# Attention inside one hybrid decoder layer on one core: the sink as a score column, earlier copies of transposed weights, one block without Strassen

## The chip, the cores and the metric

The kernel runs on one core of one Trainium2 chip. The metric is the device time of one execution in microseconds (us), lower is better.

## The reference

One layer of a decoder trunk for 512 tokens of width 1024, all in float32. An input projection feeds two branches, sliding-window attention (A) and gated linear attention (GLA, B); gates mix them; a SwiGLU block and a per-layer embedding block follow. The part that the change touches is A, with 8 query heads in 2 groups, 128-token blocks and a window of 128, and the projection of q and k for B:

```python
q_a, k_a, v_a, q_g, k_g, v_g, gk_low, og, gate_a, gate_g = jnp.split(h @ w_in, points, axis=-1)
...
s = jnp.einsum('bnqhgd,bnkhd->bnhgqk', qb, kb) * (HEAD_DIM ** -0.5)
s = s + band_relative_bias(rel_table)
dist = (jnp.arange(BLOCK)[:, None] + BLOCK) - jnp.arange(2 * BLOCK)[None, :]
in_window = (dist >= 0) & (dist < WINDOW)
...
s = jnp.where(valid[None, :, None, None], s, -1e30)
m = jnp.maximum(jnp.max(s, axis=-1, keepdims=True), sink)
pr = jnp.exp(s - m)
denom = jnp.sum(pr, axis=-1, keepdims=True) + jnp.exp(sink - m)
o = jnp.einsum('bnhgqk,bnkhd->bnqhgd', pr / denom, vb)
```

The sink is one number per head that joins the maximum and the denominator and has no value vector. A query at place q of its block sees the keys of the block before at places above q only, so the first key of the block before (column 0 of 256) is outside the window for every query.

## The kernel before

Matmuls run in three products of fp32r halves: `split` makes a high part (`_h`, a CAST on ACT, line 111) and a low part (`_l`, a TENSOR_TENSOR on DVE or POOL, line 112), and `mm3` (lines 122 to 124) issues high by high, low by high, high by low. Weights arrive by DMA from the SP queue into four raw tiles, are split into four slots (`wh`, `wl`) and are used in the order of the list `units`.

Two ways to multiply a block of 256 output columns by the 1024 inputs and 512 tokens exist. `fm_pair` is the plain one: 2 output halves by 8 input tiles by 3 matmuls of 512 tokens. `quad_pair` is Strassen's scheme in Winograd's form: seven quarter products of 4 by 3 matmuls of 256 tokens, named by four parts .0 to .3, with sums of weight quarters made on POOL (`sums_to`, line 237; tiles `qk0.0s`, `qk1.0s`, two tiles per block in two buffers) and with sums of the activation quarters `h_t` made once on DVE and ACT for all blocks. One running PSUM bank (`qk0pa`) collects the products; after each part ACT copies it to SBUF (`copy`, line 549; tiles `qk0u`, `qk0v`), and the next part's matmuls into that bank wait for that copy. DVE adds the pieces (line 545). The q and k of GLA are the blocks qk0 to qk3, its output gate the blocks og0 to og3.

Attention (`attention`, from line 714) has eight items j (block n of four, group g of two). Each is cut in steps: `scores` (matmuls into `sc`, two evictions with scale and bias on DVE into `s_all`, then the softmax), `transposes` (four or eight on PE into `pt`, one or two copies on ACT to `pT`), `values` (matmuls into `pov`). The softmax of an item is, in order: maximum of the scores (`mx`, DVE line 746), minimum of its negative with the negated sink (`nm`, 749), sink plus that (`dl`, 751), its exponential (`es`, ACT 753), four exponentials of the scores with sums (`su`, ACT 756), sum plus `es` (`de`, DVE 758), reciprocal (`rd`, 760), four scalings (ACT 762).

The steps are interleaved by hand: `drive(gla_qk(), att)` advances attention by one step after each quarter part of a qk block, `drive(gla_gate((0, 1)), att)` goes on with og0 and og1. A scheduler then sets the order of each engine's queue from program order and its own estimates; each engine runs its queue strictly in that order. `high_priority` puts an instruction ahead in that scheduler's eyes. Ahead of qk0 on all engines stand the attention queries' blocks qa0 and qa1, whose low parts for the two groups are tiles `qa<-qa,qs` (DVE for group 0, POOL for group 1), copied by DMA to `qs`.

```python
    att = attention()
    drive(gla_qk(), att)
    drive(gla_gate((0, 1)), att)
```

Of the kernel before, what the change touches and what calls it, by code (L numbers as in the profile page):

```python
# [9 lines left out]
F32 = mybir.dt.float32  # L10
F32R = mybir.dt.float32r
U8 = mybir.dt.uint8
AF = mybir.ActivationFunctionType
ALU = mybir.AluOpType
AX = mybir.AxisListType

P = 128
S = 512
D = 1024
NT = S // P  # L20
KD = D // P
# [6 lines left out]
C_QG, C_KG, C_VG = 768, 1280, 1792  # L28
# [5 lines left out]
def hybrid_layer(  # L34
# [26 lines left out]
    nc = tc.nc  # L61
    x = x[0]
    out = out[0]
# [10 lines left out]
    sm = ctx.enter_context(tc.tile_pool(name="sm", bufs=4))  # L74
# [11 lines left out]
    def t2(name, shape=(P, 512), dt=F32):  # L86
        return tp.tile(list(shape), dt, tag="t2", name=name)
# [54 lines left out]
    def u_rows(name, mat, k0, n, c0, ncol=512, per=2):  # L142

        for u in range(n // per):
            k = k0 + per * u
            units.append((f"{name}{u}", (per, ncol), [((ALL,), mat[:, k : k + per, c0 : c0 + ncol])]))
# [16 lines left out]
    for i in range(2):  # L163
        for kh in range(2):
# [2 lines left out]
                c0 = C_QA + (4 * g + 2 * i) * 64  # L167
                pieces.append(((ALL, ALL, slice(128 * g, 128 * g + 128)), wk[:, 4 * kh : 4 * kh + 4, c0 : c0 + 128]))
            units.append((f"qa{i}{kh}", (4, 256), pieces))
    for i in range(4):  # L170
        u_quad(f"qk{i}", wk, C_QG + 256 * i)
    for i in range(4):
        u_quad(f"og{i}", wk, C_OG + 256 * i)
# [296 lines left out]
    bgk = cpool.tile([P, 4], F32, name="bgk")  # L470
    glag = cpool.tile([P, 2], F32, name="glag")
    sink = cpool.tile([P, 8], F32, name="sink")
    nsink = cpool.tile([P, 8], F32, name="nsink")
    rt = cpool.tile([32, 8], F32, name="rt")
    oh = t2("oh")
    band = t2("band")
# [15 lines left out]
    with tc.issue_after(done):  # L492
        nc.vector.tensor_copy(rts, rt.unsqueeze(1).broadcast_to([32, 16, 8]))
        nc.vector.tensor_scalar_mul(glag, glag, 0.5)
        nc.vector.tensor_scalar_mul(nsink, sink, -1.0)
        nc.vector.tensor_scalar_mul(nbgk, bgk, -1.0)
        nc.vector.tensor_copy(masks, mraw)

# [82 lines left out]
    def fm_pair(name, act, evac):  # L581

        pss = [bank(f"{name}p{x}") for x in "ab"]
        for kh in range(2):
            w = W.take(f"{name}{kh}")
            for e in range(2):
                fm_mms(pss[e], w, tok(e), act, 4 * kh, 4, kh == 0, kh == 1)
                if kh:
                    evac(e, pss[e])
                yield  # L590
# [124 lines left out]
    def attention():  # L715
        items = [(n, g) for n in range(NT) for g in range(2)]
        pov = {}
        pTs = {}

        def spans(n):  # L720
            nk = 1 if n == 0 else 2
            return nk, nk * P, (n + 1 - nk)

        def scores(j):
            n, g = items[j]
            nk, w, kb = spans(n)
            rows = slice(64 * g, 64 * g + 64)
            s = s_all[:, j % 2, :, :w]
            for pair in range(2):
                ps = bank(f"sc{j}{pair}").rearrange("p (a b) -> p a b", a=2)  # L730
                keys = slice(kb * P, (n + 1) * P)
                for a in range(2):
                    h = 2 * pair + a
                    if n == 0:
                        nc.tensor.matmul(ps[:, a, :w], lhsT=qa[rows, h, tok(n)], rhs=k_aT[rows, 0:P], start=True, stop=True)
                        continue
                    q = qs[g][:, h, tok(n)]
                    nc.tensor.matmul(ps[:, a, :w], lhsT=q, rhs=ks[g][:, keys], start=True, stop=False)
                    nc.tensor.matmul(ps[:, a, :w], lhsT=q, rhs=kl[g][:, keys], start=False, stop=True)
                hs = slice(g * 4 + 2 * pair, g * 4 + 2 * pair + 2)  # L740
                nc.vector.scalar_tensor_tensor(
                    out=s[:, 2 * pair : 2 * pair + 2, :], in0=ps[:, :, :w], scalar=0.125, in1=bias[:, hs, 256 - w : 256],
                    op0=ALU.mult, op1=ALU.add,
                )
            mx = sm.tile([P, 4], F32, tag="mx", name=f"mx{j}")
            nc.vector.tensor_reduce(out=mx, in_=s, axis=AX.X, op=ALU.max, negate=True)
            sk = sink[:, 4 * g : 4 * g + 4]
            nm = sm.tile([P, 4], F32, tag="nm", name=f"nm{j}")
            nc.vector.tensor_tensor(out=nm, in0=mx, in1=nsink[:, 4 * g : 4 * g + 4], op=ALU.min)  # L749
            dl = sm.tile([P, 4], F32, tag="dl", name=f"dl{j}")  # L750
            nc.vector.tensor_tensor(out=dl, in0=sk, in1=nm, op=ALU.add)
            es = sm.tile([P, 4], F32, tag="es", name=f"es{j}")
            nc.scalar.activation(es, dl, AF.Exp)
            su = sm.tile([P, 4], F32, tag="su", name=f"su{j}")
            for a in range(4):
                nc.scalar.activation(s[:, a, :], s[:, a, :], AF.Exp, bias=nm[:, a : a + 1], accum_out=su[:, a : a + 1])  # L756
            de = sm.tile([P, 4], F32, tag="de", name=f"de{j}")
            nc.vector.tensor_add(de, su, es)
            rd = sm.tile([P, 4], F32, tag="rd", name=f"rd{j}")
            nc.vector.reciprocal(rd, de)  # L760
            for a in range(4):
                nc.scalar.activation(s[:, a, :], s[:, a, :], AF.Copy, scale=rd[:, a : a + 1])  # L762

        def transposes(j):
            n, g = items[j]
            nk, w, kb = spans(n)
            s = s_all[:, j % 2, :, :w]
            pTs[j] = []
            for b in range(nk):
                pst = bank(f"pt{j}{b}")  # L770
                for a in range(4):
                    nc.tensor.transpose(out=pst[:, tok(a)], in_=s[:, a, tok(b)], identity=ident)
                pT = t2(f"pT{j}{b}")
                nc.scalar.copy(pT, pst)  # L774
                pTs[j].append(pT)

        def values(j):
            n, g = items[j]
            nk, w, kb = spans(n)
            rows = slice(64 * g, 64 * g + 64)  # L780
            if g == 0:
                pov[n] = bank(f"pov{n}")
            for b in range(nk):
                nc.tensor.matmul(  # L784
                    pov[n][rows, :], lhsT=v_a[:, kb + b, rows], rhs=pTs[j][b], start=(b == 0), stop=(b == nk - 1)
                )
            del pTs[j]
            if g:
                split(oaT.part(0, ALL, tok(n)), pov[n].rearrange("p (t q) -> p t q", t=4))

        for j in range(len(items) + 1):
            if j < len(items):
                scores(j)
                yield
            if j == 1:

                yield
            if j:
                transposes(j - 1)
                yield  # L800
                values(j - 1)
                if j != 2:
                    yield
# [4 lines left out]
    sild = dram.tile([8, P, 512], F32, name="sild")  # L808

    def gla_qk():  # L810
        for i in range(4):
            yield from quad_pair(f"qk{i}", hT, [kq[i % 2][:, e, 1 - i // 2, :] for e in range(2)], lambda e: None)

    def gla_gate(pairs):
# [548 lines left out]
```

## Time and profile before

| | |
|---|---|
| Median of 3 runs | 885.09 us (883.25, 885.09, 885.2) |
| The profiled execution: its time, and its span | 883.18 us, 881.4 us |
| PE busy (matmul) | 855.3 us, 97% of the span |
| PEld (weight load, beside PE) | 751.7 us, 85% |
| DVE busy | 580.0 us, 66% |
| ACT busy | 454.4 us, 52% |
| POOL busy | 256.1 us, 29% |
| Mean granted TensorE clock | 0.996 of full speed |
| Chain that ended last, by engine | PE 79%, DVE 11%, ACT 4%, issue 3% |

A busy share is the mean of stages with different limits. A wait is put to whichever engine released it last. Matmuls overlap, so the distance between the starts of two matmuls in a row, not the duration of one, is what each costs. Idle time of an engine that no one waits for costs nothing.

### The profile page before, as it was taken

The numbers are of one execution on the slowest core, as the hardware profiler recorded it, in microseconds if no ns is written. First come the engines' busy times: TensorE is split into PE (matmuls) and PEld (weight loads), VectorE is DVE, ScalarE is ACT, GpSimd is POOL, SyncE is SP. The second block draws the span as 40 slices with busy tenths as digits, with TensorE's granted clock in tenths as the row PEclk, the third lists the DMA queues.
The fourth block names the chain that finished last, engine by engine and source line by source line (L and its number), as shares of the span: only waits on it lengthen the run. The fifth ranks groups of instructions, "written<-read, shape, count | busy, mean of one in ns | idle before, by whom it ended". The sixth has DMA issues, their size and how long they took to land.

```text
span 881.4 us, 15106 instructions
## 1 busy us (share of the span) xinstructions
PE 855.3 (97%) x5937; PEld 751.7 (85%) x5937; DVE 580.0 (66%) x840; ACT 454.4 (52%) x898; POOL 256.1 (29%) x211
## 2 busy tenths in 40 slices
PE   9999989999999999999998999999999999999996
PEld 7977887879777788888887999889999889998886
DVE  5534986669876634256378899535998436984574
ACT  6337767766755544333255655314555314553553
POOL 4333574331111200100033465024662034620001
PEclk9999999999999999999999999999999999999999
DMA  9482332234654337874214233431333423343402
GB/s 279 125 207 83 114 109 73 72 109 127 197 180 156 121 120 239 290 259 143 96 48 168 89 103 97 144 96 50 100 114 100 141 73 96 93 144 123 168 1 95
DMA packets 88246, 113.30 MB, mean 129 GB/s; under 512 B 6152, under 2 KB 64304, under 8 KB 87792
## 3 DMA queue, kind: packets, MB, share of 16 engines
q1 hardware_dynamic: 86704, 107.43, 38.4%
q0 software_dynamic: 1456, 4.92, 2.0%
q8 instruction: 46, 0.75, 0.3%
q14 instruction: 24, 0.20, 0.1%
q10 hardware_dynamic: 16, 0.00, 0.0%
HBM read 95.35 MB, written 15.93 MB: 126 GB/s over the span
## 4 chain that ended last, share of the span: by engine, by line
PE 79%; DVE 11%; ACT 4%; issue 3%; DMA 1%; SPq 1%; POOL 0%; POOLq 0%; DVEq 0%; ACTq 0%
DVE u L1242 2%; PE pov L784 1%; PE lv L877 1%; DVE h_t L112 1%; PE yaps L122 1%; PE yaps L124 1%; PE gt0ps L122 1%; PE gt0ps L124 1%; PE wo0ps L122 1%; PE yaps L123 1%; PE fo00ps L122 1%; PE fo10ps L123 1%; PE gt0ps L123 1%; PE wo0ps L124 1%; PE wo0ps L123 1%
## 5 line engine op out<-in xcount | busy, mean ns | idle before, releaser
L308 POOL TENSOR_TENSOR or<-om,mhalf 128x1 f32<-128x1 f32 x16 | 12.3, 770 | 64.7 <-DVE om L312 64.7
L111 ACT CAST act_h<-u 128x512 fp32r<-128x512 f32 x22 | 13.7, 621 | 27.4 <-DVE u L1242 27.4
L1242 DVE TENSOR_TENSOR u<-u,g 128x512 f32<-128x512 f32 x22 | 25.7, 1169 | 0.4
L869 DVE TENSOR_TENSOR zs<-zs,kq 128x512 f32<-128x512 f32 x28 | 19.8, 723 | 5.8 <-ACT zs L865 5.8
L308 POOL TENSOR_TENSOR h20r<-h20n,mhalf 128x1 f32<-128x1 f32 x1 | 0.6, 562 | 72.1 <-DVE h20n L317 72.1
L961 ACT ACTIVATE own<-o,or 128x256 f32<-128x256 f32 x16 | 7.6, 475 | 18.6 <-POOL or L308 18.5
L784 PE MATMUL pov<-pT,kv 128*64 128x512 f32 x28 | 14.4, 612 | 2.9 <-ACT pT L774 2.9
L756 ACT ACTIVATE s_all<-s_all,nm 128x256 f32<-128x256 f32 (+1 forms) x32 | 15.1, 472 | 3.2 <-DVE nm L749 3.2
L863 DVE TENSOR_TENSOR zs<-G 128x512 f32<-128x512 f32 x24 | 15.8, 684 | 0.4 <-DMA G<-Gd 0.4
L762 ACT ACTIVATE s_all<-s_all,rd 128x256 f32<-128x256 f32 (+1 forms) x32 | 13.2, 473 | 5.4 <-DVE rd L760 5.3
L112 DVE TENSOR_TENSOR act_l<-u,act_h 128x512 fp32r<-128x512 f32 x22 | 14.9, 680 | 0.0
L1239 ACT ACTIVATE g<-g 128x512 f32<-128x512 f32 x22 | 13.9, 631 | 0.3
L122 PE MATMUL yaps<-qs,pa_h 128*128 128x512 f32 x32 | 13.6, 426 | 0.0
L864 ACT ACTIVATE zs<-zs 128x256 f32<-128x256 f32 x28 | 11.7, 419 | 3.6 <-DVE zs L863 3.2
L111 ACT CAST mx_h<-yg 128x512 fp32r<-128x512 f32 x8 | 5.0, 622 | 15.5 <-DVE yg L1077 15.5
L122 PE MATMUL v1ps<-v_h,h_h 128*128 128x512 f32 x32 | 12.9, 403 | 0.0
L122 PE MATMUL gt0ps<-gt_h,xT_h 128*128 128x512 f32 x32 | 12.9, 402 | 0.0
L122 PE MATMUL wo0ps<-wo_h,mx_h 128*128 128x512 f32 x32 | 12.7, 395 | 0.0
L122 PE MATMUL wo1ps<-wo_h,mx_h 128*128 128x512 f32 x32 | 12.6, 394 | 0.0
L124 PE MATMUL yaps<-qs,pa_l 128*128 128x512 f32 x32 | 12.6, 394 | 0.0
L124 PE MATMUL gt0ps<-gt_h,xT_l 128*128 128x512 f32 x32 | 12.5, 391 | 0.0
L124 PE MATMUL v1ps<-v_h,h_l 128*128 128x512 f32 x32 | 12.5, 390 | 0.0
(2556 smaller groups left out, 3680.7 us busy)
## 6 DMA issues: line engine op xcount, KB each, us to landing
mg<-mgd SPq DMA_DIRECT2D x8, 512.0 KB, 5.8
vd<-v_g SPq DMA_DIRECT2D x2, 1024.0 KB, 4.8
sild<-gw SPq DMA_DIRECT2D x8, 256.0 KB, 2.1
own<-vd SPq DMA_DIRECT2D x4, 512.0 KB, 5.3
own<-sild SPq DMA_DIRECT2D x4, 512.0 KB, 5.1
mgd<-gw SPq DMA_DIRECT2D x8, 256.0 KB, 2.4
ogd<-og SPq DMA_DIRECT2D x8, 256.0 KB, 3.8
mgd<-sgg SPq DMA_DIRECT2D x8, 256.0 KB, 3.9
```

The costliest lines, as they stand in the source:

```text
L111: ins = nc.scalar.copy(hi, src)
L112: eng.tensor_tensor(out=lo, in0=src, in1=hi.bitcast(F32), op=ALU.subtract)
L122: nc.tensor.matmul(ps, lhsT=l[0], rhs=r[0], start=first, stop=False, **kw)
L123: nc.tensor.matmul(ps, lhsT=l[0], rhs=r[1], start=False, stop=False, **kw)
L124: nc.tensor.matmul(ps, lhsT=l[1], rhs=r[0], start=False, stop=last, **kw)
L756: nc.scalar.activation(s[:, a, :], s[:, a, :], AF.Exp, bias=nm[:, a : a + 1], accum_out=su[:, a : a + 1])
L762: nc.scalar.activation(s[:, a, :], s[:, a, :], AF.Copy, scale=rd[:, a : a + 1])
L784: nc.tensor.matmul(pov[n][rows, :], lhsT=v_a[:, kb + b, rows], rhs=pTs[j][b], start=(b == 0), stop=(b == nk - 1))
L863: pe.tensor_tensor(out=z3, in0=g3, in1=g3[:, :, b - 1 : b].broadcast_to([P, nb, 2 * b]), op=ALU.subtract)
L869: nc.vector.tensor_tensor(out=d4, in0=d4, in1=kq_, op=ALU.mult)
L1239: nc.scalar.activation(gs[e], gs[e], AF.Silu)
L1242: nc.vector.tensor_tensor(out=us[e], in0=us[e], in1=gs[e], op=ALU.mult)
```

## The change

Three edits, all in the code around attention.

The sink becomes one more column of the scores: it is copied into `s_all` (column 0, which the window always masks, or column 128 for the first block, which has 128 keys), so the maximum and the exponentials' sums take it in. `nsink`, `mx`, `dl`, `es` and `de` go, and with them four DVE instructions and one on ACT per item, and one DVE copy of 128x4 comes. Since column 0 then holds a probability, the values of the block before are taken from `v_z`, a copy of `v_a` with row 0 zeroed, made once on POOL.

The copies `pT` get priority 300. The block qk0 is multiplied by `fm_pair` in place of `quad_pair`; its evacuations are two copies on ACT.

```diff
-    for i in range(4):
+    u_rows("qk0", wk, 0, KD, C_QG, 256, 4)
+    for i in range(1, 4):
         u_quad(f"qk{i}", wk, C_QG + 256 * i)
...
-    nsink = cpool.tile([P, 8], F32, name="nsink")
...
+        v_z = t2("v_z", (P, NT, P))
+        nc.gpsimd.tensor_copy(v_z, v_a)
+        nc.gpsimd.memset(v_z[0:1], 0.0)
...
-            mx = sm.tile([P, 4], F32, tag="mx", name=f"mx{j}")
-            nc.vector.tensor_reduce(out=mx, in_=s, axis=AX.X, op=ALU.max, negate=True)
-            sk = sink[:, 4 * g : 4 * g + 4]
+            at = 0 if nk == 2 else w
+            nc.vector.tensor_copy(s_all[:, j % 2, :, at], sink[:, 4 * g : 4 * g + 4])
+            s = s_all[:, j % 2, :, : max(w, at + 1)]
             nm = sm.tile([P, 4], F32, tag="nm", name=f"nm{j}")
-            nc.vector.tensor_tensor(out=nm, in0=mx, in1=nsink[:, 4 * g : 4 * g + 4], op=ALU.min)
-            dl = sm.tile([P, 4], F32, tag="dl", name=f"dl{j}")
-            nc.vector.tensor_tensor(out=dl, in0=sk, in1=nm, op=ALU.add)
-            es = sm.tile([P, 4], F32, tag="es", name=f"es{j}")
-            nc.scalar.activation(es, dl, AF.Exp)
+            nc.vector.tensor_reduce(out=nm, in_=s, axis=AX.X, op=ALU.max, negate=True)
...
-            de = sm.tile([P, 4], F32, tag="de", name=f"de{j}")
-            nc.vector.tensor_add(de, su, es)
             rd = sm.tile([P, 4], F32, tag="rd", name=f"rd{j}")
-            nc.vector.reciprocal(rd, de)
+            nc.vector.reciprocal(rd, su)
...
-                nc.scalar.copy(pT, pst)
+                with tc.high_priority(offset=300):
+                    nc.scalar.copy(pT, pst)
...
-                    pov[n][rows, :], lhsT=v_a[:, kb + b, rows], ...
+                    pov[n][rows, :], lhsT=(v_z if b < nk - 1 else v_a)[:, kb + b, rows], ...
...
     def gla_qk():
-        for i in range(4):
+        yield from fm_pair("qk0", hT, lambda e, ps: nc.scalar.copy(kq[0][:, e, 1, :], ps))
+        for i in range(1, 4):
```

The order of the queues moves between about 84 and 197 us of the span; after og1 it is the same as before on every engine. Three places matter below.

POOL, from the low part of the attention keys to the sums of qk2; `qk1.0s` are the sums for block qk1, `qk1.0_l` and `qk0.3_l` low parts of weights, `qa` the low parts of the queries of group 1. Before:

```order
L237 TENSOR_TENSOR qk1.0s_930<-qk1r_812,qk1r_852 128x512
L112 TENSOR_TENSOR qa<-qa,qs_889 64x2x384
L237 TENSOR_TENSOR qk1.0s_930<-qk1.0s_930,qk1r_812 128x512
L112 TENSOR_TENSOR qk0.3_l<-qk0r_741,qk0.3_h 128x512
L237 TENSOR_TENSOR qk1.0s_931<-qk1r_852,qk1.0s_930 128x512
L237 TENSOR_TENSOR qk1.0s_931<-qk1r_812 128x512
L112 TENSOR_TENSOR qa<-qa,qs_889 64x2x384
```

Now:

```order
L720 COPY v_z<-kv 128x512
L721 MEMSET v_z 1x512
L238 TENSOR_TENSOR qk1.0s_840<-qk1r_804,qk1r_838 128x512
L238 TENSOR_TENSOR qk1.0s_841<-qk1r_804 128x512
L238 TENSOR_TENSOR qk1.0s_840<-qk1.0s_840,qk1r_804 128x512
L238 TENSOR_TENSOR qk1.0s_841<-qk1r_838,qk1.0s_840 128x512
L112 TENSOR_TENSOR qk1.0_l<-qk1r_838,qk1.0_h 128x512
L112 TENSOR_TENSOR qa<-qa,qs_887 64x2x384 x2
```

All of qk0's own work has left POOL, the sums of qk1 stand together, and the queries' low parts come behind them.

ACT, from the split of the second pair of queries (`qs`) to the copy `pT` of the first item. Before:

```order
L756 ACT_TABLE_LOAD
L756 ACTIVATE s_all,su_1027<-s_all,nm_1021 128x128
L753 ACTIVATE es_1025<-dl_1023 128x4
L756 ACTIVATE s_all,su_1027<-s_all,nm_1021 128x128 x3
L111 CAST qk1.1_h<-qk1.0s_930 128x1024
L762 ACTIVATE s_all<-s_all,rd_1034 128x128 x3
L549 COPY qk0v<-qk0pa 128x256
```

Now:

```order
L111 CAST qk1.1_h<-qk1.0s_840 128x1024
L111 CAST qs_886<-qa 64x2x384
L111 CAST qs_887<-qa 64x2x384
L756 ACT_TABLE_LOAD
L756 ACTIVATE s_all,su_1004<-s_all,nm_1002 128x129 x4
L111 CAST qk1.2_h<-qk1.0s_841 128x1024
L760 ACTIVATE s_all<-s_all,rd_1009 128x128 x4
L756 ACTIVATE s_all,su_1038<-s_all,nm_1036 128x129 x4
L810 COPY kq_965<-qk0pa 128x512
L760 ACTIVATE s_all<-s_all,rd_1043 128x128 x4
L810 COPY kq_965<-qk0pb 128x512
L773 COPY pT_1090<-pt_1085 128x512
```

The cast `qk1.1_h`, which reads a sum that POOL makes, now stands ahead of the first item's whole softmax, and no copy of the running bank stands among the scalings.

ACT around the copies `pT` of the fifth item (pt_1697 and pt_1704 before, pt_1595 and pt_1602 now), whose reader is the value product. Before:

```order
L111 CAST og0.2_h<-og0.0s_1522 128x1024
L756 ACTIVATE s_all,su_1647<-s_all,nm_1641 128x256
L753 ACTIVATE es_1645<-dl_1643 128x4
L756 ACTIVATE s_all,su_1647<-s_all,nm_1641 128x256 x2
L549 COPY kq_974<-qk3pa 128x256
L774 COPY pT_1702<-pt_1697 128x512
L774 COPY pT_1709<-pt_1704 128x512
```

Now:

```order
L111 CAST og0.2_h<-og0.0s_1427 128x1024
L773 COPY pT_1600<-pt_1595 128x512
L773 COPY pT_1607<-pt_1602 128x512
L756 ACTIVATE s_all,su_1547<-s_all,nm_1545 128x256 x2
L548 COPY kq_966<-qk3pa 128x256
```

The two copies moved ahead of the next item's exponentials.

## Rows read from the trace of the kernel before

**Rows 1.** Waits of PE, whole span: us in total, times, longest.

```profile
PE qk0pa L122 <- ACT qk0v L549: 3.2, 1, 3.2
PE pov L784 <- ACT pT L774: 2.9, 2, 1.6
PE fg00pc L122 <- DVE h2t L1110: 2.1, 1, 2.1
...
PE pt L772 <- ACT s_all L762: 0.9, 1, 0.9
```

**Rows 2.** Busy time by stretch: PE, PEld, DVE, ACT, POOL, clock, DMA.

```profile
110.00:132.00 22.00, 19.52 (x135) 17.63 (x136) 19.05 (x27) 14.80 (x43) 16.94 (x13) 0.92 0.37 111
...
462.00:484.00 22.00, 18.60 (x120) 16.52 (x119) 19.05 (x26) 12.43 (x24) 6.86 (x5) 1.00 0.52 176
```

**Rows 3.** Timeline of PE, qa1 to qk1: start, duration, instruction, [idle before].

```profile
87.07 0.39 PE L122 MATMUL qa1pa<-h_h,qa_h 128*128 128x512 f32 x1
...
97.95 0.28 PE L122 MATMUL qk0pa<-h_h,qk0.0_h 128*128 128x256 f32 x1
...
100.70 0.28 PE L124 MATMUL qk0pb<-h_h,qk0.0_l 128*128 128x256 f32 x1
...
112.47 0.39 PE L122 MATMUL qk0pa<-h_t,qk0.3_h 128*128 128x256 f32 x1 [3.19 <-ACT qk0v L549]
...
118.93 1.07 PE L784 MATMUL pov<-pT,kv 128*64 128x512 f32 x2
119.94 0.38 PE L122 MATMUL qk1pa<-h_t,qk1.1_h 128*128 128x256 f32 x1
```

**Rows 4.** Timeline of ACT, same stretch.

```profile
96.73 1.69 ACT L111 CAST qs<-qa 64x768 fp32r<-64x768 f32 x2
...
104.12 1.28 ACT L756 ACT_TABLE_LOAD   x1
...
108.34 0.39 ACT L756 ACTIVATE s_all<-s_all,nm 128x128 f32<-128x128 f32 x1
...
109.49 1.03 ACT L111 CAST qk1.1_h<-qk1.0s 128x1024 fp32r<-128x1024 f32 x1
111.18 0.99 ACT L762 ACTIVATE s_all<-s_all,rd 128x128 f32<-128x128 f32 x3 [0.66 <-DVE rd L760]
```

**Rows 5.** Timeline of DVE, same stretch.

```profile
99.88 1.21 DVE L112 TENSOR_TENSOR qk0.2_l<-qk0.0s,qk0.2_h 128x1024 fp32r<-128x1024 f32 x1
101.06 1.98 DVE L112 TENSOR_TENSOR qa<-qa,qs 64x768 fp32r<-64x768 f32 x1
...
106.13 0.69 DVE L746 TENSOR_REDUCE mx<-s_all 128x4 f32<-128x512 f32 x1
...
109.62 1.05 DVE L758 TENSOR_TENSOR de<-su,es 128x4 f32<-128x4 f32 x1 [0.76 <-ACT s_all L756]
```

**Rows 6.** Timeline of POOL, same stretch.

```profile
84.88 1.29 POOL L112 TENSOR_TENSOR qk0.0_l<-qk0r,qk0.0_h 128x512 fp32r<-128x512 f32 x1 [11.96 <-ACT qk0.0_h L111]
98.17 4.06 POOL L237 TENSOR_TENSOR qk1.0s<-qk1r,qk1r 128x512 f32<-128x512 f32 x1 [12.00 <-ACT qs L111]
...
109.38 1.27 POOL L237 TENSOR_TENSOR qk1.0s<-qk1r 128x512 f32<-128x512 f32 x1
```

**Rows 7.** Groups by line and form, 84 to 205 us: busy us, mean ns, idle.

```profile
L741 DVE SCALAR_TENSOR_TENSOR s_all<-sc,bias 128x256 f32<-128x256 f32 x4 | 1.6, 406 | 0.0
```

**Rows 8.** Timeline of PE, the fifth and the seventh item's value products.

```profile
162.70 1.93 PE L784 MATMUL pov<-pT,kv 128*64 128x512 f32 x4 [1.59 <-ACT pT L774]
...
189.41 1.07 PE L784 MATMUL pov<-pT,kv 128*64 128x512 f32 x2 [1.26 <-ACT pT L774]
```

**Rows 9.** Timeline of ACT up to the fifth item's two copies.

```profile
158.78 1.05 ACT L111 CAST og0.2_h<-og0.0s 128x1024 fp32r<-128x1024 f32 x1 [0.99 <-PE qk3pb L123]
...
162.07 1.05 ACT L774 COPY pT<-pt 128x512 f32<-128x512 f32 x2
```

**Rows 10.** Instructions that write dcy, a DVE copy of 128x4: duration min/median/max ns.

```profile
L913 DVE COPY dcy<-eg x4: 160/162/1007, 208.6 to 281.0; 128x4 f32<-128x4 f32 x4
```

More of the change, by code (lines that the diff above doesn't have):

```diff
@@ L494, in hybrid_layer @@
         nc.vector.tensor_scalar_mul(glag, glag, 0.5)
-        nc.vector.tensor_scalar_mul(nsink, sink, -1.0)
         nc.vector.tensor_scalar_mul(nbgk, bgk, -1.0)
@@ L756, in scores @@
                 nc.scalar.activation(s[:, a, :], s[:, a, :], AF.Exp, bias=nm[:, a : a + 1], accum_out=su[:, a : a + 1])
-            de = sm.tile([P, 4], F32, tag="de", name=f"de{j}")
-            nc.vector.tensor_add(de, su, es)
             rd = sm.tile([P, 4], F32, tag="rd", name=f"rd{j}")
-            nc.vector.reciprocal(rd, de)
+            nc.vector.reciprocal(rd, su)
             for a in range(4):
-                nc.scalar.activation(s[:, a, :], s[:, a, :], AF.Copy, scale=rd[:, a : a + 1])
+                nc.scalar.activation(s[:, a, :w], s[:, a, :w], AF.Copy, scale=rd[:, a : a + 1])
         def transposes(j):
@@ L784, in values @@
                 nc.tensor.matmul(
-                    pov[n][rows, :], lhsT=v_a[:, kb + b, rows], rhs=pTs[j][b], start=(b == 0), stop=(b == nk - 1)
+                    pov[n][rows, :], lhsT=(v_z if b < nk - 1 else v_a)[:, kb + b, rows], rhs=pTs[j][b], start=(b == 0), stop=(b == nk - 1)
                 )
```

## The prediction

> **What bounds the kernel now.** The page says that PE is busy for 97% of the span, so a change shortens the run only by taking work off PE or by taking away a time in which PE stands. The list of waits shows where it stands [rows 1]: the longest is 3.2 us before the last part of qk0, then two waits of the value products, 2.9 us in all, and 0.9 us before a transpose. All of these lie in the stretch that the change rewrites. The timelines give their places: the 3.19 us end at 112.47 [rows 3], the value products wait 1.59 and 1.26 us [rows 8], which with the 0.9 make 6.9 us.
>
> The first wait has a second price. The table by stretch shows a granted clock of 0.92 between 110 and 132 us [rows 2]: part of it ran at the lower of the two levels, 1.2 in place of 2.4 GHz. That is (1 - 0.92) x 22 = 1.76 us of work lost right behind the 3.19 us wait. Between 462 and 484 us PE stands 22 - 18.6 = 3.4 us in several waits, the longest 2.1 [rows 1, 2], and the clock there is 1.00: not every wait of this kind is followed by the lower level.
>
> Why did PE wait? ACT had the copy of the running bank (`qk0v`) behind three scalings that began at 111.18 after 0.66 us of waiting for `rd` [rows 4]. That came behind `de`, which took 1.05 us on DVE [rows 5] for four numbers per partition. These small DVE instructions with two inputs are long where POOL works at the same time: the one at 109.62 lasts as long as the sum that POOL began at 109.38 [rows 5, 6].
>
> **qk0 plainly: more columns.** 48 matmuls of 512 tokens replace 84 of 256. The 48 of qa1 take from 87.07 to 97.95, 10.88 us. The first 24 of qk0 start from 97.95 to 100.70, so one of 256 costs 2.75 / 23 = 0.1196 us and 84 cost 10.05 [rows 3]. PE pays **+0.83 us**. Score matmuls and the switches between kinds of matmul stay as many. The running bank goes, and with it the 3.19 us wait (3.35 by the starts, since a gap of 0.12 would be normal) and, if nothing as long replaces it, the 1.76 us of lower clock: **-5.1 us** gross.
>
> **What is late next.** The order of ACT and POOL moves in a way that gives some of it back. The cast `qk1.1_h` now stands ahead of the second pair of query casts, the table load and the first softmax, and needs the third of POOL's sums for qk1. When does POOL make them? In the trace of before its first such sum is open from 98.17 and lasts 4.06 us, where an undisturbed one lasts 1.27 [rows 6]: it got through only about 101, when DVE paused between two instructions [rows 5]. In the change DVE has the same chain of two-input instructions up to about 101.2 (weights, sums of activations, a query part; it was busy to 101.06 before [rows 5]), and then itself waits for `qk1.1_h`. So I take POOL's start there. Step by step, with durations of [rows 4 to 7]: three sums at 1.27, 105.0; `qk1.1_h` 1.03, 106.0; two query casts 1.69, 107.7, while DVE waits out POOL's fourth sum, makes `qk1.1_l` (1.2) and the second query part (0.9, the 1.98 of [rows 5] less a sum's hold) until 108.3; two evictions at 0.41 and the maximum at 0.69, 109.7; the table load ended at 109.0 and is hidden; four exponentials at (109.49 - 108.34) / 3 = 0.38, 111.2; `qk1.2_h`, 112.2; four scalings at 0.33, 113.5.
>
> PE meanwhile: 97.95 + 10.88 + 2.5 for two groups of scores = 111.3 (before, 112.47 - 3.19 - 97.95 = 11.33 us held 72 matmuls of qk0, 8.6, the same two groups, and 0.2 of a last matmul's tail [rows 3]). So the first transposes wait for the scalings, about **+2.2 us**, and end at 113.8; 24 matmuls of qk1, 116.7. ACT goes on with four exponentials (115.0), a copy of 0.52 (half of the 1.05 in [rows 9]), four scalings and a second copy, then `pT` at 117.9: the first value product waits **+1.2 us**, runs 1.0 and lets qk1.1 start at 118.9. Before it started at 119.94 [rows 3]. This part therefore gains **1.0 us**, of the 5.1, if the clock holds; 2.2 us of standing is nearer to the 2.1 without a lower clock behind it than to the 3.19 with one, so I take it to hold.
>
> **The later items.** `pT` priority: at the fifth item the copies came at 162.07, behind the next item's exponentials, and PE waited 1.59 us [rows 8, 9]. They now stand ahead of them, right behind a cast that ends at 159.83 [rows 9], so they can end at 160.9, and PE comes at 161.1: the wait goes. The seventh item has the same pattern, and its 1.26 us go. At the third item the transposes waited 0.9 us for scalings that waited for `rd`; without `de`, and with the reciprocal ahead of the next maximum, some 0.2 is left. Value products that were issued one by one (1.07 each [rows 3], with work between) now come in pairs, 1.93 per pair [rows 8]: 0.2 for each of three items. Sum **-4.1 us**.
>
> **Edits at nothing.** The dropped `nsink`, `dl`, `es` and qk0's adds ease DVE and ACT, which are less busy than PE. `v_z` and its memset fall into the 12 us in which POOL idles before 84.88 [rows 6]; if POOL were late there, each would cost 1.3. The sink's copy is a DVE copy of 128x4; the four in GLA take from 0.16 to 1.01 us [rows 10]. I take 0.2, the median's end, since it stands where POOL has mostly finished its sums; at 1.0 it would return most of the third item's 0.7, and nothing elsewhere, where the scalings have over 2 us in hand. Past og1 the order is unchanged and PE has no wait that the change touches, so what is gained by then is kept to the end.
>
> **Sum.** -1.0 - 4.1 = **-5.1 us** against the profiled execution's 883.18, or 878.1. Of the four executions shown two lie near 883.2 and two near 885.1, the median 885.09 is one of the upper. From their middle, 884.15, the forecast is **879.0 us**.
>
> **Rivals.**
> - *POOL comes earlier* (20%). If DVE pauses once or twice between 95 and 101 us, the sums for qk1 are ready before ACT asks. Then no wait of 2.2 at the transposes and little at the value product: the first part gains 3.35 + 1.76 - 0.83 - 0.5 = 3.8. For it: POOL's queue is free of qk0. Against: the 4.06 us [rows 6]. 876.2 us.
> - *The clock falls again* (15%), behind a wait of 2.2 to 3 us at the first transposes: 1.76 us more, 880.8.
> - *The later waits only move* (12%). ACT's freed time is filled by exponentials that now come behind `pT`, and scalings or the copies of running banks come late in their turn; half of the 4.1 us is lost and some of the first part: 881.5 to 882.5.
> - *POOL takes its turn after every DVE instruction* (8%), slower than before. From about 96 us its four sums, a weight part and two query parts (1.27 to 1.8 each, 9.9 us) would stand between the nine DVE instructions ahead of the first eviction, which then comes at 113.5 in place of 108.3. The first transposes end at about 119 and not 113.8, the clock falls with so long a wait (1.8 or more), and qk1.1 starts near 125 plus that, 7 us later than before; less 4.1 that is 887. It decides from the point at which the first scalings end after 117. Against it: the sum open at 98.17 was passed by the DVE instruction of 99.88 [rows 5, 6].
>  The Trainium skill (SBUF — State Buffer, "Who interferes with whom") says that issue order decides which of DVE and GpSimd blocks when both want the shared port pair. Read as a strict order of requests, it would have given the port to the sum opened at 98.17 ahead of the instruction of 99.88; the trace shows otherwise. By that reading the result would be this rival's 887, by the row the forecast's 879.0.
>
> That the change does not do what it says is no case here: the order of the queues shows all three edits.
>
> **How the numbers follow.** The forecast has 45%. Its own bounds are 877 to 881 (the sink's copy, the waits of 2.2 and 1.2 by 1 us each way, the two groups of executions). About 0.3% (2.65 us) is what a measurement of this kernel can tell from no change; faster by more needs under 882.4 against the median shown. Forecast, earlier POOL, the second clock fall and part of the moved waits lie below: 0.80. The rest of the moved waits, 0.12. Slower: 0.08. The range 875.0 to 882.5 leaves out the slow rival, and the tails of the others.
>
> **What would show it.** PE's list of waits should have no `qk0pa`; in its place a wait of about 2 us at the first `pt` and one of about 1 us at the first `pov`, and none above 0.5 at later `pov`. The stretch 110 to 132 should show a clock of 1.00. ACT's cast `qk1.1_h` should start near 105 and be released by POOL. qk1.1 should start near 118.9, and og2 some 5 us earlier than before. The forecast is wrong if the first scalings end before 111.5 (better) or after 115 (worse), or if a lower clock shows.

## The result and the profile after

The changed kernel takes 877.85 us in the median of four runs (877.11 to 878.55), the kernel before 885.05 beside it: 0.9935 of the time, with a 95% interval of 0.9923 to 0.9947. The forecast was 879.0 in a range of 875.0 to 882.5. The profiled execution took 877.55 us with a span of 875.7, against 883.18 and 881.4. Three of the four executions of the kernel before lie between 885.0 and 885.2 and one at 883.25, so the medians are 7.2 us apart and the two profiled executions 5.6.

The first part of the page, busy time, share of the span and instructions:

```profile
PE 854.3 (98%) x5901; PEld 749.2 (86%) x5901; DVE 569.8 (65%) x818; ACT 450.3 (51%) x885; POOL 251.9 (29%) x207
```

PE's waits after, which answer to [rows 1] (us in total, times, longest), between 90 and 330 us:

```profile
PE pov L783 <- ACT pT L773: 1.0, 1, 1.0
PE o L953 <- ACT sc L968: 0.7, 1, 0.7
PE pt L770 <- ACT s_all L760: 0.7, 1, 0.7
```

The 3.2 us before `qk0pa`, the 2.9 in two waits at later value products and the 0.9 at later transposes are gone. What stays (`pt` and `pov`) is at the first item, and one wait is new: a value product `o` of a linear attention head, far behind the change. By stretch, as [rows 2]:

```profile
110.00:132.00 22.00, 20.34 (x143) 17.31 (x142) 14.38 (x21) 16.96 (x50) 15.61 (x11) 1.00 0.41 109
132.00:154.00 22.00, 22.00 (x160) 18.81 (x159) 13.56 (x21) 17.50 (x45) 9.85 (x7) 1.00 0.26 72
```

The clock between 110 and 132 is 1.00 in place of 0.92, and in the stretch behind it PE is busy without a gap. PE's timeline at the first item, as [rows 3]:

```profile
112.40 1.21 PE L770 MATMUL pt<-ident,s_all 128*128 128x128 f32 x4 [0.70 <-ACT s_all L760]
...
117.42 1.07 PE L783 MATMUL pov<-pT,kv 128*64 128x512 f32 x2 [0.95 <-ACT pT L773]
```

ACT, DVE and POOL there, as [rows 4 to 6]:

```profile
103.16 1.05 ACT L111 CAST qk1.1_h<-qk1.0s 128x1024 fp32r<-128x1024 f32 x1 [3.06 <-POOL qk1.0s L238]
...
111.95 1.27 ACT L760 ACTIVATE s_all<-s_all,rd 128x128 f32<-128x128 f32 x4
```

```profile
96.58 1.22 DVE L112 TENSOR_TENSOR qk_l<-qk01r,qk_h 128x1024 fp32r<-128x1024 f32 x1
97.93 2.10 DVE L112 TENSOR_TENSOR h_t<-hr,h_t 128x1024 fp32r<-128x1024 f32 x1
99.95 2.03 DVE L112 TENSOR_TENSOR qa<-qa,qs 64x768 fp32r<-64x768 f32 x1
...
103.61 1.32 DVE L750 COPY s_all<-sink 128x4 f32<-128x4 f32 x2
...
107.95 0.74 DVE L744 SCALAR_TENSOR_TENSOR s_all<-sc,bias 128x256 f32<-128x256 f32 x2
```

```profile
95.96 2.98 POOL L238 TENSOR_TENSOR qk1.0s<-qk1r,qk1r 128x512 f32<-128x512 f32 x1 [38.71 <-DMA qk1r<-in_w_in]
98.91 2.26 POOL L238 TENSOR_TENSOR qk1.0s<-qk1r 128x512 f32<-128x512 f32 x1
101.14 1.99 POOL L238 TENSOR_TENSOR qk1.0s<-qk1.0s,qk1r 128x512 f32<-128x512 f32 x1
```

From 97.8 us POOL's sums and DVE's two-input instructions take turns: the three DVE instructions shown first end at 97.80, 100.03 and 101.98, and the sums 1.14 us behind each, at 98.94, 101.17 and 103.13. A sum is open for 2 to 3 us where an undisturbed one lasts 1.27 [rows 6], and a DVE instruction of the size of the one at 96.58 grows from 1.22 to 2.10.

**A ledger of PE.** The starts of four matmuls in PE's timeline cut every profiled execution into stretches: the first of qk1.1, of og2, of ga3 (a gate's block, behind the new wait) and of wo0 (the output projection). From ga3 to wo0 all thirteen profiles have 112.0 us, and they differ behind wo0 too, with the clock, as the end of this document shows. So the start of wo0, not the span, is the sharper measure of what an edit did in the execution that was profiled; it is used below beside the times. It is one execution of each kernel, and not always a typical one. Where qk1 is plain there is no qk1.1.

| kernel | qk1.1 | to og2 | og2 to ga3 | wo0 |
|---|---|---|---|---|
| before | 119.94 | 77.59 | 102.49 | 412.03 |
| changed | 118.42 | 72.43 | 103.50 | 406.35 |
| changed, again (c_after) | 118.47 | 72.42 | 103.82 | 406.71 |
| plain qk0 alone (e1) | 122.42 | 77.46 | 102.51 | 414.41 |
| without plain qk0 (e2) | 120.77 | 72.44 | 102.50 | 407.71 |
| without priority (e3) | 118.17 | 73.74 | 102.52 | 406.43 |
| without sink column (e4) | 122.27 | 73.36 | 103.59 | 411.24 |
| sink column alone (e7) | 121.26 | 74.65 | 102.46 | 410.37 |
| qk1 plain too (e5) | | og2 at 189.16 | 103.39 | 404.56 |
| own late (e6) | 118.78 | 72.43 | 102.86 | 406.07 |
| e5 and e6 together (e8) | | og2 at 189.01 | 103.39 | 404.40 |
| the same without priority (e9) | | og2 at 189.79 | 103.55 | 405.35 |
| e1 with es late (e10) | 120.39 | 75.66 | 102.51 | 410.57 |

The change gained 1.52 us up to qk1.1, 5.16 from there to og2, and gave back 1.01 before ga3: 5.67 in all.

### The profile page after: what moved, and what is told of

It reads as the page before. It is cut to its first block, busy times and chain, and to the rows that moved or that the text cites. A ratio compares the mean times of both kernels' runs of the same rounds, so it can differ in the third digit from the quotient of the medians.

```text
span 875.7 us, 14980 instructions
## 1 busy us (share of the span) xinstructions
PE 854.3 (98%) x5901; PEld 749.2 (86%) x5901; DVE 569.8 (65%) x818; ACT 450.3 (51%) x885; POOL 251.9 (29%) x207
## 4 chain that ended last, share of the span: by engine, by line
PE 79%; DVE 9%; issue 4%; ACT 4%; DMA 2%; POOL 1%; SPq 1%; POOLq 0%; DVEq 0%; ACTq 0%
DVE u L1242 2%; PE pov L783 2%; PE v1ps L122 1%; PE gt0ps L124 1%; PE v1ps L123 1%; PE wo0ps L124 1%; PE gt0ps L122 1%; PE v1ps L124 1%; PE gt0ps L123 1%; PE fo10ps L122 1%; PE fo00ps L122 1%; PE wo0ps L122 1%; PE fo10ps L123 1%; PE fo00ps L123 1%; PE wo0ps L123 1%
## 5 line engine op out<-in xcount | busy, mean ns | idle before, releaser
L238 POOL TENSOR_TENSOR qk1.0s<-qk1r,qk1r 128x512 f32<-128x512 f32 x1 | 3.0, 2984 | 38.7 <-DMA qk1r<-in_w_in 38.7
```

## The experiments

Times are medians, each beside the kernel before on the same chip (883.39 us for e1 to e4, 884.24 for c_after and e5 to e7, 883.30 for e8 to e10), ratios with their 95% intervals.

### Which edit pays: e1, e2, e3, e4, e7

**e1**, of the diff above only the plain block:

```diff
-    for i in range(4):
+    u_rows("qk0", wk, 0, KD, C_QG, 256, 4)
+    for i in range(1, 4):
         u_quad(f"qk{i}", wk, C_QG + 256 * i)
...
```

> The kernel before with qk0 multiplied plainly and nothing else. Theory (each edit pays its own part): the wait of qk0pa (3.2 us) and the lower clock behind it (1.76 us) go, but the small instructions dl, es and de stay in the chain of the first softmax, and one of them took 1.05 us before, so the first transposes wait 1.7 to 3.2 us in place of the 0.70 of the changed kernel; the later waits of the value products (1.59 and 1.26) and of the transposes (0.9) stay as before. First part between 0.5 better and 1.0 worse than before: 883 to 886 us. Rival (the plain block carries the gain): 880 us or less, with first waits as short as in the changed kernel. Second rival (the wait at the first transposes passes 3 us and the clock falls again): 886 to 888 us, and a granted clock under 0.95 between 110 and 132 us.

888.25 us, 1.0048 (1.0034 to 1.0061): slower, as the second rival had it (0.25 us above its range). PE's waits, the longest of them, and the stretch:

```profile
PE pt L773 <- ACT s_all L763: 4.4, 2, 3.6
PE pov L785 <- ACT pT L775: 2.8, 2, 1.6
```

```profile
115.25 1.36 PE L773 MATMUL pt<-ident,s_all 128*128 128x128 f32 x4 [3.64 <-ACT s_all L763]
```

```profile
110.00:132.00 22.00, 18.36 (x112) 15.71 (x110) 14.16 (x22) 13.78 (x41) 11.89 (x9) 0.84 0.40 109
```

The wait of 3.2 us became one of 3.6 in another place, with more of the lower clock behind it. Why, the timelines of DVE and ACT show:

```profile
109.56 1.77 DVE L752 TENSOR_TENSOR dl<-sink,nm 128x4 f32<-128x4 f32 x1
...
112.76 1.26 DVE L759 TENSOR_TENSOR de<-su,es 128x4 f32<-128x4 f32 x1 [0.76 <-ACT s_all L757]
```

```profile
111.37 0.21 ACT L754 ACTIVATE es<-dl 128x4 f32<-128x4 f32 x1 [1.31 <-DVE dl L752]
...
114.80 1.28 ACT L763 ACTIVATE s_all<-s_all,rd 128x128 f32<-128x128 f32 x4 [1.14 <-DVE rd L761]
```

The first exponential begins at 109.56, within 0.11 us of the changed kernel's 109.45, but the scalings 2.85 us later. `dl`, four numbers per partition, takes 1.77 us on DVE beside POOL's low parts of the queries (107.07 to 111.3); the second item's `dl`, while POOL does nothing, takes 0.15. ACT, which has `es` behind the first exponential, stands 1.31 us for the long one, and 1.14 more for `rd`, behind a `de` of 1.26.

**e2**, the change with qk0 left to Strassen's scheme:

```diff
-    u_rows("qk0", wk, 0, KD, C_QG, 256, 4)
-    for i in range(1, 4):
+    for i in range(4):
         u_quad(f"qk{i}", wk, C_QG + 256 * i)
...
```

> The changed kernel with qk0 multiplied by Strassen's scheme again; sink column and priority stay. Theory: without es and de the scalings of the first item end 1 to 1.5 us earlier, so the wait of qk0pa shrinks from 3.2 to about 2 us, and a wait of 2 us may leave the clock at 1.00; the later waits stay away (-4.1 us against before). 879 to 881.5 us. Rival (the plain block carries the gain): qk0pa waits 3 us again with a clock of about 0.92, 882 us or more. Second rival (the plain block is worth nothing, sink and priority do all): 877.5 to 878.5 us.

879.2 us, 0.9953 (0.9940 to 0.9967), in the theory's range; by the trace the wait before `qk0pa` is 1.17 us, where the theory had about 2. But a wait of 2.54 us at a matmul of qk1, for the low part `qk1.0_l` from POOL, and a clock of 0.92 between 110 and 132 make qk1.1 later than before all the same:

```profile
116.84 0.39 PE L124 MATMUL qk1pb<-h_h,qk1.0_l 128*128 128x256 f32 x1 [2.54 <-POOL qk1.0_l L112]
```

**e3**, the change without the priority:

```diff
-                with tc.high_priority(offset=300):
-                    nc.scalar.copy(pT, pst)
+                nc.scalar.copy(pT, pst)
```

> The changed kernel with the copies of the transposed weights at their usual priority. In the order the second copy of the third and of the fifth item falls back behind exponentials or scalings of the next item, the first item's copy stays. Theory (the priority removed the waits of 1.59 and 1.26 us): two or three value products wait 1 to 1.6 us again, 879.5 to 882 us. Rival (the sink column alone frees ACT enough): no wait above 0.5 us at later value products, 877.5 to 878.5 us.

879.7 us, 0.9954 (0.9940 to 0.9967); the time is in the expected range, but the trace holds no wait at a later value product, only these two, at the first item:

```profile
PE pov L782 <- ACT pT L772: 1.0, 1, 1.0
PE pt L770 <- ACT s_all L760: 0.7, 1, 0.7
```

The stretch to og2 is 1.3 us longer than with the priority, and all but 0.08 of the difference at wo0 is gone, because here nothing is lost at `o`. The 1.3 us are in PE's order. The two value products of the third item, here with other matmuls between them and with the priority in a row:

```profile
135.83 1.07 PE L782 MATMUL pov<-pT,v_z 128*64 128x512 f32 x2
...
137.50 1.07 PE L782 MATMUL pov<-pT,kv 128*64 128x512 f32 x2
```

```profile
136.09 1.07 PE L783 MATMUL pov<-pT,v_z 128*64 128x512 f32 x2
137.00 1.02 PE L783 MATMUL pov<-pT,kv 128*64 128x512 f32 x2
```

At the fifth and the sixth item they stand 2.27 and 2.99 us apart in place of 0.91. So the theory's reason fell in this execution: beside the sink column those waits are gone without the priority too (e7, below, agrees). What the time shows is less clear. The profiled execution, 878.10, is the fastest of five; two others took 879.28 and 879.90 with a mean granted clock of 0.998 against its 0.996. What cost them 1.2 and 1.8 us more this trace does not show.

**e4**, the plain block and the priority, the sink as before:

```diff
-    for i in range(4):
+    u_rows("qk0", wk, 0, KD, C_QG, 256, 4)
+    for i in range(1, 4):
...
-                nc.scalar.copy(pT, pst)
+                with tc.high_priority(offset=300):
+                    nc.scalar.copy(pT, pst)
...
```

> The kernel before with qk0 plain and the copies at priority 300, the sink handled as before. Theory: the first transposes wait 1 to 2.5 us longer than the 0.70 us of the changed kernel, since dl, es and de stand in the chain beside a busy POOL, and the wait of 0.9 us at the third item's transposes stays: 879.5 to 881.5 us. Rival (the sink column is worth nothing, since its own copy takes 1.32 us twice beside POOL): 877.5 to 878.5 us.

882.98 us, 0.9990 (0.9979 to 1.0001): nearly the whole gain is lost, more than expected. The first transposes wait as in e1, and the clock of 110 to 132 is 0.84:

```profile
115.30 1.36 PE L773 MATMUL pt<-ident,s_all 128*128 128x128 f32 x4 [3.65 <-ACT s_all L763]
```

The later waits of value products are gone here too, this time by the priority. (The rival's 1.32 us are the sink's two copies together, not each.)

**e7**, the sink column alone: e3 with the edit of e2.

```diff
-    u_rows("qk0", wk, 0, KD, C_QG, 256, 4)
-    for i in range(1, 4):
+    for i in range(4):
...
-                with tc.high_priority(offset=300):
-                    nc.scalar.copy(pT, pst)
+                nc.scalar.copy(pT, pst)
...
```

> The kernel before with the sink column alone: qk0 by Strassen's scheme, usual priority. If the parts add up as the other runs have them: qk1.1 starts about 0.8 us later than before (as with sink and priority), the stretch from there to og2 is 3.9 us shorter (as with sink and plain block), nothing is lost behind: 3.0 us less than before in the profiled execution, 879.5 to 881 us, ratio about 0.9965. Rival (the priority is needed for the later waits in this order): a wait above 1 us at a later value product, 882 us or more. Second rival (the sink carries everything): under 878.5 us.

880.6 us, 0.9960 (0.9948 to 0.9973), in the theory's range. No value product between 90 and 330 us waits 0.5 us or more. The parts are a little off: qk1.1 starts 1.3 us later than before and the next stretch is 2.9 us shorter, not 3.9. The lower clock accounts for that: it lasts past qk1.1 (0.67 between 122 and 124 us), which by the granted clock costs this stretch about 1.0 us.

What follows: the sink column carries most of the gain. Alone it takes 0.4% of the time away (e7), and what is left without it (e4) is not told apart from nothing. The plain block makes the kernel 0.5% slower on its own; at wo0 it gains 1.4 us beside the sink column and the priority (e2 to the change) and 3.9 beside the sink column alone (e7 to e3), which the times of those two do not show. The priority beside the sink column is worth 0.1 us at wo0 with the plain block (e3 to the change) and 2.7 without it (e7 to e2), part of it e7's longer lower clock; the priority alone was not run.

From qk1.1 to og2, beside a plain qk0, the sink column alone saves 3.7 us (e1 to e3), the priority alone 4.1 (e1 to e4), both 5.0. The waits account for this: either edit takes away the two of the value products, 2.8 us together; the third item's wait at `pt`, 0.8 or 0.9, stays in e4 and goes only with the sink column; the 1.3 us of value products in a row come only with the priority.

### Why the plain block alone loses: e10

e1, with `es` behind the four exponentials in ACT's order:

```diff
-            nc.scalar.activation(es, dl, AF.Exp)
             su = sm.tile([P, 4], F32, tag="su", name=f"su{j}")
...
             de = sm.tile([P, 4], F32, tag="de", name=f"de{j}")
+            nc.scalar.activation(es, dl, AF.Exp)
             nc.vector.tensor_add(de, su, es)
```

> The kernel before with qk0 plain alone, and the exponential of the sink (es) put behind the four exponentials of the scores in ACT's order, where before it stood behind the first of them. Theory (the small two-input instructions dl and de on DVE beside a busy POOL make the plain block's first softmax late): of the 1.31 us for which ACT waited for dl only 0.5 to 0.9 come back, since de still waits for dl and es; the first transposes wait 2.7 to 3.1 us in place of 3.64 and the clock still falls: 885.5 to 887.5 us by the scale on which the plain block alone had 888. Rival (the place of es in ACT's queue is the cause): the wait falls by 1.3 us or more, to 2.3 us or less, the clock stays at 1.00 between 110 and 132 us, and the time is 884 us or less.

883.82 us, 0.9999 (0.9988 to 1.0009). The wait, and ACT:

```profile
113.91 1.36 PE L773 MATMUL pt<-ident,s_all 128*128 128x128 f32 x4 [2.30 <-ACT s_all L763]
```

```profile
111.37 0.20 ACT L757 ACTIVATE es<-dl 128x4 f32<-128x4 f32 x1 [0.16 <-DVE dl L752]
```

`dl` takes 1.78 us as before, but ACT stands 0.16 for it and not 1.31, and PE 2.30 in place of 3.64. That is the rival's size: the place of `es` in a strict queue cost 1.3 us. Of the clock the rival was wrong: 0.92 between 110 and 132 us, where e1 has 0.84. In the two traces, moving a 0.2 us instruction three places makes wo0 start 3.84 us earlier: 2.03 up to qk1.1, and 1.80 behind, where one of the two waits of value products is gone.

### The turns of POOL and DVE at the first item: c_after, e5

c_after is the change itself, on the chip of e5 to e7.

> The changed kernel itself, on the same chip as the three that follow, as their measure. Expected 0.9935 of the time before (interval of the first measurement 0.9923 to 0.9947): 876.5 to 879.5 us, a wait of 0.7 at the first transposes, 1.0 at the first value product and 0.7 at a value product o of the third head.

877.46 us, 0.9923 (0.9910 to 0.9937), as expected but for the wait at `o`, 1.0 us here.

**e5** multiplies qk1 plainly as well:

```diff
-    for i in range(1, 4):
+    u_rows("qk1", wk, 0, KD, C_QG + 256, 256, 4)
+    for i in range(2, 4):
         u_quad(f"qk{i}", wk, C_QG + 256 * i)
...
+        yield from fm_pair("qk1", hT, lambda e, ps: nc.scalar.copy(kq[1][:, e, 1, :], ps))
-        for i in range(1, 4):
+        for i in range(2, 4):
```

> The changed kernel with qk1 multiplied plainly as well, so that POOL makes no sums and no low parts of weights while DVE prepares the first softmax. Theory (the alternation of POOL and DVE, about 1 us on each of five DVE instructions, is what makes the first transposes and the first value product late): the first evictions come some 3 us before 107.95, the waits of 0.70 and 0.95 go, PE pays 0.83 us of columns: 0.8 us less than the changed kernel. Rival (ACT's own queue makes them late): both waits stay and the columns are paid, 0.8 us more. Second rival (the steps of attention fall on longer pieces of qk1 and a later wait appears): 1 to 3 us more, with a wait at the second item.

876.51 us, 0.9917 (0.9905 to 0.9930). DVE, and PE between 90 and 330 us:

```profile
97.67 1.22 DVE L112 TENSOR_TENSOR h_t<-hr,h_t 128x1024 fp32r<-128x1024 f32 x1
98.81 0.94 DVE L112 TENSOR_TENSOR qa<-qa,qs 64x768 fp32r<-64x768 f32 x1
...
103.31 0.74 DVE L745 SCALAR_TENSOR_TENSOR s_all<-sc,bias 128x256 f32<-128x256 f32 x2
```

```profile
PE o L955 <- ACT sc L970: 0.6, 1, 0.6
```

Without POOL's sums for qk1 the instructions that took 2.10 and 2.03 take 1.22 and 0.94, the first evictions come 4.6 us earlier, and neither the transposes nor the first value product wait. og2 starts 1.73 us earlier than in c_after although the columns of a second plain block are paid. Of the 4.6 us, 2.0 are these two instructions, whose turns with POOL are gone. The rest is order: the low part `qk1.1_l`, made from POOL's sums, and the sink's copy no longer stand ahead of the evictions. So what POOL makes for qk1 was behind the two remaining waits; how much of them the turns alone would have cost was not separated. The time is lower by 0.95 us in the median, but the two intervals overlap: the gain is shown in the trace and not in the time.

### What took 1.0 us back behind og2: e6, e8, e9

The changed kernel's chain to the new wait, against before: POOL's power `or` (128x1), which waits for nothing but `om`, in the kernel before:

```profile
258.37 1.06 POOL L308 TENSOR_TENSOR or<-om,mhalf 128x1 f32<-128x1 f32 x1 [3.76 <-DVE om L312]
...
264.23 0.55 POOL L308 TENSOR_TENSOR or<-om,mhalf 128x1 f32<-128x1 f32 x1 [0.69 <-DVE om L312]
```

and after:

```profile
251.86 1.66 POOL L309 TENSOR_TENSOR or<-om,mhalf 128x1 f32<-128x1 f32 x1 [3.21 <-DVE om L313]
...
258.73 0.93 POOL L309 TENSOR_TENSOR or<-om,mhalf 128x1 f32<-128x1 f32 x1 [1.68 <-DVE om L313]
```

PE is 6.67 us ahead of before in this stretch, `or` 6.51 at its first start, 5.91 at that one's end, and 5.12 at the second's end, since it takes 0.6 and 0.4 longer. In DVE's timeline the reason is a turn missed: before, the first `or` ends 0.41 us after the first of two DVE instructions in a row (which ends at 259.02), now 0.40 after the second (253.12); the second `or` came 0.1 us ahead of a DVE instruction before, and 0.16 behind it now. Both first ones began 0.03 to 0.04 us behind the same DVE instruction, so why the turn was missed is not shown. ACT's copies `own` wait for it, behind them the cast `pa_h` (265.83 before, 260.70 after: 5.13), the weight load that needs the freed slot, and in the same queue the load of `G` (issued at 272.50 and 267.39: 5.11). What needs `G` is then 5.1 to 5.6 us earlier, not 6.67, and so is the copy `sc` that PE's `o` needs.

**e6** puts `own` back in ACT's order; PE and POOL keep theirs:

```diff
-            nc.scalar.activation(v_[:, c, :], po[:, 0:256], AF.Copy, scale=r)
+            with tc.high_priority(offset=-400):
+                nc.scalar.activation(v_[:, c, :], po[:, 0:256], AF.Copy, scale=r)
```

> The changed kernel with the scaled copies of the outputs of the linear attention heads (the copies own, on ACT) put back behind their neighbours in ACT's order; PE and POOL keep their orders. Theory (a power of 128x1 on POOL, longer beside DVE, holds ACT at such a copy, and through the cast pa_h, the freed weight slot and the queue behind it delays the load of G, and so the value product o of the third head): the wait of 0.7 us before o goes and ga3 comes 0.8 to 1.0 us earlier against the start of ga2; 0.9 us less than the changed kernel. Rival (the load of G is late by its own transfer): the wait stays, no change.

877.62 us, 0.9929 (0.9916 to 0.9941): no difference from c_after that the time shows. In the trace the wait at `o` is gone, and PE's waits between 90 and 330 us are

```profile
PE pt L770 <- ACT s_all L760: 1.1, 1, 1.1
PE pov L783 <- ACT pT L773: 1.0, 1, 1.0
```

og2 to ga3 takes 102.86 us, 0.64 and 0.96 less than in the two profiles of the change, and 0.37 more than before; 0.3 to 0.4 us of it is lost again at the first item, which the edit does not touch.

**e8** is e5 with the edit of e6:

```diff
-            nc.scalar.activation(v_[:, c, :], po[:, 0:256], AF.Copy, scale=r)
+            with tc.high_priority(offset=-400):
+                nc.scalar.activation(v_[:, c, :], po[:, 0:256], AF.Copy, scale=r)
```

> qk0 and qk1 plain, sink column and priority, and the copies own put back in ACT's order as in the run before. Theory (the two gains lie at different places and add up): no wait of PE in attention and none at o; the first wo0 matmul starts about 0.6 us earlier than the 404.56 of the run with qk1 plain, and 2.4 to 3.0 us earlier than the 406.35 and 406.71 of the changed kernel. 875 to 876 us. Rival (without the waits ahead of it the third head meets another late transfer): the wait at o stays or moves, 876.5 us or more.

876.38 us, 0.9922 (0.9909 to 0.9935). The wait at `o` stands at 0.6 as in e5, in a head that comes earlier (between 215 and 240 us): the rival's case. The gains do not add up; wo0 is only 0.16 us earlier than in e5. What holds that earlier head was not tried.

**e9** is e8 with the edit of e3:

```diff
-                with tc.high_priority(offset=300):
-                    nc.scalar.copy(pT, pst)
+                nc.scalar.copy(pT, pst)
```

> The same kernel without the priority of the copies of transposed weights. Theory (with the sink column the priority is worth what the stretch from qk1.1 to og2 showed, 73.74 us without it and 72.43 with it, and nothing behind takes it back here): 1.0 to 1.3 us more than the same kernel with the priority. Rival (the priority is worth nothing beside the sink column, as the whole time of the changed kernel without it showed in the trace): within 0.3 us of it.

876.86 us, 0.9929 (0.9917 to 0.9942), not told apart in time; wo0 starts 0.95 us later. So here, beside two plain blocks, the priority is worth about a microsecond in the trace, a little less than expected.

e5 and e8 are the best versions found: wo0 starts 1.8 to 2.3 us earlier than in the two profiles of the change. In time neither is told apart from it: e5 lies 0.95 us below c_after in the median, and the ratio of e8 (0.9922) is that of c_after (0.9923).

## Why the prediction was right, and where not

- **What the plain block costs PE.** Right to 0.2 us: the last of qk0's matmuls starts at 111.31, and one of them takes 0.23 from start to start, where the forecast had PE at the first transposes at 111.3. The 3.19 us wait and its lower clock went.
- **When POOL makes the sums for qk1.** This step failed. "I take POOL's start there", at 101.2: the first sum was done at 98.9 and the third at 103.1, not 105.0. The start rested on a pause of DVE at about 101 in the kernel before; in [rows 5] the two instructions there follow without a gap (99.88 + 1.21 = 101.09, the next at 101.06). Now POOL took turns with DVE from 97.8, so `qk1.1_h` began at 103.16 and not 105. But the same turns stretched four DVE instructions by 0.9 to 1.1 us each, and the first evictions came at 107.95, where 108.3 was forecast, the scalings' end at 113.2 (113.5). Two errors cancelled, by luck. The rival of the turns was right in its mechanism and wrong in its size (it had the evictions at 113.5). The rival of an earlier POOL had its condition right, DVE did pause once at 97.8, but not its price, since it left out what POOL's turns cost DVE. The Trainium skill (SBUF — State Buffer, "Who interferes with whom") has issue order decide. The second and third sums agree with that; the first, open from 95.96, was passed by the DVE instruction of 96.58, as the one of 98.17 was in the kernel before [rows 5, 6].
- **First waits.** Forecast 2.2 and 1.2; measured 0.70 and 0.95. The first is short in the list because a transpose starts with each scaling that is ready: the four take 1.21 us, and the next matmul of qk1 starts at 113.36, 0.4 us ahead of the forecast. qk1.1 came at 118.42 (118.9): this part gained 1.5 and not 1.0.
- **The clock holds.** Right for this kernel, in both of its profiles, but not by its argument: the wait at the first transposes that was taken to leave the clock alone, 2.2 us, was only 0.70. In e10 PE waits 2.30 us at that place, and the clock behind it falls (0.92).
- **The later items.** -4.1 forecast, -5.16 measured, and the reason was half wrong. "`pT` priority: ... the wait goes" is what e4 shows beside the old sink. Beside the sink column the traces of e3 and e7 have no such wait without the priority. Two edits remove the same waits, and the sum gave all of it to one. Value products in a row, taken at 0.6 us for three items, were worth 1.3 (e3 to the change).
- **The sink edit at next to nothing.** "The dropped `nsink`, `dl`, `es` and qk0's adds ease DVE and ACT, which are less busy than PE" is the step that failed most. The new chain was costed without them, so the total came out; but their absence is what the change lives on. With them the plain block is slower than before (e1), and without the column the change gains 0.1%, with an interval that includes none (e4).
- **The sink's copy.** 0.2 us taken, with bounds of 0.16 and 1.01; at the first item the two copies take 1.32 together beside POOL, 0.66 each and nearer to the upper bound, ahead of `qk1.1_l`.
- **"so what is gained by then is kept to the end".** Failed by 1.0 us: an unchanged order behind og2 was taken for unchanged waits.
- **The time.** The sum had 878.1 for the profiled execution, which took 877.55: 0.5 and 1.1 us too little gain in two stretches, 1.0 us too little loss in the third. That the total came so close is in part luck.

## What to carry to other kernels

Before pricing small instructions at nothing, follow who stands behind them in a strict queue: four numbers per partition took 1.8 us on DVE beside POOL, ACT waited for them, PE waited for ACT, and the lower clock came behind PE's wait. Edits that attack the same wait must be priced together, not one by one; in one stretch the gain of each alone was 3.7 and 4.1 us, of both 5.0. And a stretch whose order is unchanged can still change when its start shifts: here a gain of 6.7 us ahead of it became 5.7 behind it, where POOL and DVE hinder each other.

## What the runs showed of the hardware that was not expected

The same wait of PE is followed by the lower clock in one execution and not in another of the same kernel. At the start of the feed-forward block (`fg00pc`) PE waits 2.1 or 2.2 us in every profile. The clock behind it, in the changed kernel's first profile (stretch, us, PE busy, clock, DMA):

```profile
472.00:474.00 2.00, 0.76 (x7) 1.00 0.48 105
474.00:476.00 2.00, 2.00 (x19) 1.00 1.02 359
```

and in the second (c_after):

```profile
472.00:474.00 2.00, 1.08 (x6) 0.51 0.31 68
474.00:476.00 2.00, 2.00 (x10) 0.50 0.95 322
```

The wait is 2.16 us in the first and 2.17 in the second, and another one soon behind it 1.24 and 0.92: the profile that keeps the higher clock has the more waiting. From wo0 to the end of the span the first profile takes 469.35 us, the second 471.29. Of the thirteen profiles five have 1.00 between 462 and 484 us (469.35 to 469.73 from wo0 to the end), five 0.92 (469.65 to 470.13) and three 0.84 or 0.90 (471.04 to 471.29). Such a spread fits the two groups of times of the kernel before, near 883.2 and 885.1. Of its 40 executions beside the experiments, the 20 under 883.6 us have a mean granted clock of 0.995 to 0.997, the 14 over 884.3 one of 0.992 to 0.994. Where in the span the clock was lower only the profiled executions show.

How little lets POOL go ahead of DVE. DVE's two-input instructions in a row overlap by 0.07 to 0.09 us in the records. Before the change and in e5 they stand so from about 97.7 us, and POOL's instruction waits: 4.06 us [rows 6], and in e5, until DVE paused 0.16 us at 101.04,

```profile
98.67 3.90 POOL L112 TENSOR_TENSOR qa<-qa,qs 64x768 fp32r<-64x768 f32 x1 [41.48 <-ACT qs L111]
```

In the changed kernel DVE paused 0.13 us, from 97.80 to 97.93, and from then on the two took turns although DVE left no gap. In e10 a pause of 0.02 us (97.71 to 97.73) was enough, and in the kernel before POOL got in where the overlap was 0.03 us, at 101.06. Whether such a late start lets POOL in, or is itself the mark of its having got in, the traces do not tell.
